# Two more independent products and later turns between output projection and gate/up; first weight sums on VectorE

## The chip, the cores and the metric

The kernel runs on one core of one Trainium2 chip. The metric is the device time of one execution in microseconds (us); of several runs the median counts. The engines are named as in the profile: PE is TensorE (matmuls and transposes), DVE is VectorE, ACT is ScalarE, POOL is GpSimd, SP is the engine whose queue issues the DMAs.

## The reference, cut to what matters

Two layers over 1024 tokens of width 1024, float32. The part around the change:

```python
mixed = jnp.einsum('bse,ed->bsd', jnp.concatenate([tok, mem_out], axis=-1), w_out[i])
x = x + rms_norm(mixed, norm_mix_post[i])
h = rms_norm(x, norm_ffn_pre[i])
gu = jnp.einsum('bsd,df->bsf', h, w_gu[i])          # w_gu: 1024 x 5632
f = jnp.einsum('bsf,fd->bsd', jax.nn.silu(gu[..., :D_FF]) * gu[..., D_FF:], w_down[i])
x = x + rms_norm(f, norm_ffn_post[i])
```

## The kernel before

**Precision.** Every float32 operand is split into a high part (a rounded copy by ScalarE) and a low part (the difference, by VectorE or GpSimd); a product is three matmuls, high x high, low x high, high x low (`mm3`, lines 91 to 93). A 128x128 by 128x512 step is thus three matmuls. `split_raw` (L113) splits a weight unit `wr` of 128x1024 into `wh` (L115) and `wl` (L116); `split_ps` (L95) splits what lies in PSUM.

**Output projection.** The loop of L895 takes the 8 token tiles i one after the other: 48 matmuls into two PSUM banks, then `tail` (L426): squares on ScalarE (L431), `ms` (L161) on VectorE, `r = ms^-0.5` on GpSimd (L165), two scalings (L436), the residual add (L437), the store of x (L424), and `norm_rows` (L173): squares (L176), `ms` (L163), `r`, and the normalised tile `ht` (L178). `turn_tile` (L855) turns a tile: 8 transposes (L186) into the two `pst` banks, and `put_block` copies them to `z` (L838) and splits tokens 0 to 511 into B11 and B21 and the second half of tokens 512 to 1023 into B22. For i >= 4 `combine` (L845) subtracts quarters of `z` in place, four operations of 128x512 on L853, on VectorE for tile 7 and on GpSimd else. In program order the turn of tile i-1 follows the projection of tile i.

**Gate/up.** One level of a Strassen-Winograd scheme: 2x2 blocks of tokens by inner dimension on one side, of weights on the other. A unit f has 7 products of 12 matmuls (`product`, L923): S2·T2, S1·T1, S3·T3, A11·B11, A12·B21, A22·T4 and S4·B22, where A11, A12 are the gate weights, A21, A22 the up weights, S1 to S4 four sums of them (`Sums`, L945, lines 954 to 957) and T1 to T4 what `combine` left in `z`, split in L1063 and L1064. Pieces of S and A22 are split by `piece` (L916). `gate_up` (L977) adds the products up (`add`, L975) and applies Silu. There are 22 units in the order n = 0, 1, 2, ... that is f = 0, 11, 1, 12, ...; weight unit names are w56 and w57 (gate and up of f = 0), w78 and w79 (f = 11), w58 and w59 (f = 1), w80 and w81 (f = 12). The names are those of layer 0. Raw weights come through a ring of two buffers (`load_raw`, L103).

**The junction.** B11 and B21 are complete after tile 3, so products with them can run before tiles 6 and 7 are turned. Lines 1036 to 1053 do this: the gate units w56 and w78 are loaded and split, their A11·B11 and A12·B21 computed into `ahead`, those of w58 into `kept`, the splits of S2, S1, S3, A22, S4 of unit f = 0 made (`A.all()`), and tile 7 turned. The first unit's weight sums run on GpSimd (L1040), into buffers named `attn`. Then T2, T1, T3 and T4 are split, the first two pieces of T2 and of T1 on GpSimd (TPOOL), and the units follow. Unit n = 2 takes its two products from `kept`.

**What sets the order.** Outside the attention a scheduler sorts the instructions of each engine's queue by when it expects them ready; each engine then runs its queue in order and waits on semaphores. DMA issues stand in SP's queue in the same way. Two instructions without a common tile can be ordered by a dependency without a semaphore (`add_manual_dep`).

Of the kernel before, what the change touches and what calls it, by code (L numbers as in the profile page):

```python
# [66 lines left out]
def build(nc, tc, ctx, x_in, mem_in, wts, t5, onehot, sinks, rpb, maskb, gains, out):  # L67
# [105 lines left out]
    def norm_rows(npool, xt, g, nb):  # L173
        ht = npool.tile([P, D], F32, name="ht", tag="ht", bufs=nb)
        ss = npool.tile([P, 1], F32, name="ss", bufs=4)
        nc.scalar.activation(ht, xt, AF.Square, scale=ROOT, accum_out=ss)  # L176
        r = rms(npool, [ss])
        nc.vector.scalar_tensor_tensor(ht, xt, r, g, ALU.mult, ALU.mult)  # L178
        return ht

    def turn(pspool, tag, ht, put):

# [243 lines left out]
    def tail(npool, i, parts, g1, g2, xt, dst, dgrid, nb):  # L426

        tt = npool.tile([P, D], F32, name="tt", tag="ht", bufs=nb)
        ss = npool.tile([P, 2], F32, name="ssp", bufs=4)
        for k, ps in enumerate(parts):  # L430
            nc.scalar.activation(tt[:, k * HALF:(k + 1) * HALF], ps, AF.Square, scale=ROOT,  # L431
                                 accum_out=ss[:, k:k + 1])
        r = rms(npool, [ss[:, 0:1], ss[:, 1:2]])
        for k, ps in enumerate(parts):
            ks = slice(k * HALF, (k + 1) * HALF)
            nc.vector.scalar_tensor_tensor(tt[:, ks], ps, r, g1[:, ks], ALU.mult, ALU.mult)  # L436
        nc.vector.tensor_tensor(xt, xt, tt, ALU.add)  # L437
        store_x(dst, xt, i, dgrid)
        return None if g2 is None else norm_rows(npool, xt, g2, nb)
# [180 lines left out]
    for layer in range(DEPTH):  # L620
# [234 lines left out]
        def turn_tile(i, ht):  # L855
            turn(psT, "pst", ht, put_block(i))
            if i >= 4:
                combine(i - 4)
# [36 lines left out]
        for i in range(NT):  # L895
            accs = [psO.tile([P, HALF], F32, name="acc", tag="acc") for _ in range(2)]
            now_ao, ao = ao, heads_out(i + 1) if i < NT - 1 else None
            xt = load_xt(i)
            for c0 in range(0, 8, 4):
                aH, aL = now_ao[c0 // 4]  # L900
                for c in range(4):
                    h, lo = wu[c0 + c]
                    for dh in range(2):
                        ds = slice(dh * HALF, (dh + 1) * HALF)
                        mm3(accs[dh], aH[:, c], aL[:, c], h[:, ds], lo[:, ds],
                            c0 + c == 0, c0 + c == 7)
            if prev is not None:
                turn_tile(i - 1, prev)
            prev = tail(npool, i, accs, gpost, gpre, xt, x_new, False, 3)
        oph.close()  # L910


        gph = Phase()
        gp = gph.open(sb(f"gu{layer}", side="left"))

        def piece(src):  # L916
            h = gp.tile([P, HALF], F32R, name="gh", tag="gh", bufs=5)
            nc.scalar.activation(h, src, AF.Copy)  # L918
            lo = gp.tile([P, HALF], F32R, name="gl", tag="gl", bufs=5)
            nc.vector.tensor_tensor(lo, src, h.bitcast(F32), ALU.subtract)  # L920
            return h, lo

        def product(A, B):  # L923
            acc = psO.tile([P, HALF], F32, name="acc", tag="acc")
            for kc in range(4):
                ks = slice(kc * P, (kc + 1) * P)
                mm3(acc, A[0][:, ks], A[1][:, ks], B[0][:, kc], B[1][:, kc], kc == 0, kc == 3)
            return acc
# [11 lines left out]
        def gate_unit(f):  # L940
            u = U_GU + 44 * layer + 2 * f
            gr = load_raw(u)
            return gr, split_raw(u, gr, ring, 3)
# [93 lines left out]
        spare = [stage.tile([P, S], F32, name="attn", tag="attn", bufs=2) for _ in range(2)]  # L1037
        spare = [t[:, k * HALF:(k + 1) * HALF] for t in spare for k in range(2)]
        gates = [gate_unit(0)]
        A = Sums(0, gates[0], spare.pop, nc.gpsimd)  # L1040
        gates.append(gate_unit(FH))
        for gate in gates:
            p1 = gp.tile([P, D], F32, name="p1", tag="tw", bufs=2)
# [2 lines left out]
            nc.scalar.activation(p1, product(A11, B11), AF.Copy)  # L1046
            add(c11, product(A12, B21), p1)
            ahead.append((p1, c11))
        gates.append(gate_unit(1))
        A11, A12 = ([t[:, k * HALF:(k + 1) * HALF] for t in gates[2][1]] for k in range(2))  # L1050
        kept = [product(A11, B11), product(A12, B21)]
        A.all()
        turn_tile(NT - 1, prev)
        nph.close()
        stage_ph.close()
        cB = com_ph.open(sb(f"comB{layer}", side="right"))
# [10 lines left out]
        for n in range(NF):  # L1067
            f = n // 2 + n % 2 * FH
            if n:
                gate = gates[n] if n < 3 else gate_unit(f)  # L1070
                if n == 2:
                    gate = load_raw(U_GU + 44 * layer + 2 * f), gate[1]
                A = Sums(f, gate, lambda: tmp("s"), nc.vector)
            if n < 2:
                p1, c11 = ahead[n]
            else:
                p1 = c11 = tmp("e")
                nc.scalar.activation(p1, kept.pop(0) if n == 2 else product(A.A11, B11), AF.Copy)
            act_sums(f, *gate_up(f, A, p1, c11, kept.pop(0) if n == 2 else None))
            if n and summed < FH and summed * (NF - LEAD) <= (n - 1) * FH:  # L1080
                weight_sums(summed)
                summed += 1
# [238 lines left out]
```

## Time and profile before

| | us |
|---|---|
| median of 3 runs | 2269.01 |
| lowest, highest | 2265.79, 2272.14 |
| the profiled execution | 2261.95 |
| its span | 2260.2 |
| PE busy | 2141.8 (95%) |
| DVE busy | 1513.8 (67%) |
| ACT busy | 1064.9 (47%) |
| POOL busy | 726.2 (32%) |

All trace times count from the span's start. A timeline row gives the start of an instruction, its length, its line, output and inputs, and in brackets how long its engine was idle before it and what released it. Rows of one kind that follow each other are one row with xN, whose length spans all of them. Matmuls overlap, so the pace of a row of matmuls is read from their starts. The mean granted TensorE clock is 0.983 of full speed.

### The profile page before, as it was taken

What the parts mean: (1) busy time and instruction counts of PE and PEld (TensorE: products, weight loads), DVE (VectorE), ACT (ScalarE), POOL (GpSimd) and SP (SyncE); (2) the same over time, 40 slices, a digit from 0 to 9 for tenths busy, and PEclk for the clock granted to TensorE, in tenths of its full rate; (3) what the DMA queues carried; (4) which work ended last, traced back from release to release, by engine and by line L of the source; (5) the groups of instructions that cost most, each with busy time, mean ns of one, the idle gap of its engine ahead of it and who ended that gap; (6) DMA issues with size and microseconds to landing.
All of it is one profiled execution on the core that took longest, in us unless ns stands there. A gap on an engine that the chain in (4) does not pass through costs nothing. (4 is left out here: it accounts for less than half of the span.)

```text
span 2260.2 us, 31296 instructions
## 1 busy us (share of the span) xinstructions
PE 2141.8 (95%) x10538; PEld 1779.4 (79%) x10538; DVE 1513.8 (67%) x2629; ACT 1064.9 (47%) x2162; POOL 726.2 (32%) x810
## 2 busy tenths in 40 slices
PE   7899888989999999999899999999899999999986
PEld 7678787768888888887788889777688888888865
DVE  5578785588777765556657665765877777755556
ACT  5488784442233333534457665754523333224333
POOL 3167661424333321102215342524233333211012
PEclk9999999999999999999999999999999999999998
DMA  6433445325555544856333232433255545446664
GB/s 206 118 88 91 135 135 156 98 79 189 175 183 170 180 138 162 276 193 235 114 104 97 78 87 69 132 112 107 75 180 183 184 170 177 145 146 222 193 207 164
DMA packets 152791, 336.49 MB, mean 149 GB/s; under 512 B 24727, under 2 KB 47127, under 8 KB 152632
## 3 DMA queue, kind: packets, MB, share of 16 engines
q1 hardware_dynamic: 152632, 334.50, 46.2%
q8 instruction: 84, 1.38, 0.3%
q14 instruction: 75, 0.61, 0.1%
HBM read 229.06 MB, written 95.03 MB: 143 GB/s over the span
## 5 line engine op out<-in xcount | busy, mean ns | idle before, releaser
L975 DVE TENSOR_TENSOR zt<-acc,zt 128x512 f32<-128x512 f32 x300 | 204.9, 686 | 155.9 <-PE acc L93 153.7
L1120 DVE TENSOR_TENSOR dl<-draw,dh 128x1024 fp32r<-128x1024 f32 x146 | 187.1, 1288 | 163.7 <-ACT dh L1118 163.1
L274 POOL TENSOR_TENSOR sn<-sn,st 128x384 f32<-128x384 f32 (+1 forms) x256 | 188.1, 736 | 254.3 <-DVE st L273 217.7
L1118 ACT ACTIVATE dh<-draw 128x1024 fp32r<-128x1024 f32 x146 | 154.0, 1059 | 218.5 <-PE acc L93 125.8
L92 PE MATMUL acc<-dl,dh 128*128 128x512 f32 x584 | 229.7, 393 | 14.9 <-DVE dl L1120 13.0
L93 PE MATMUL acc<-dh,dl 128*128 128x512 f32 x584 | 228.2, 391 | 0.0
L91 PE MATMUL acc<-dh 128*128 128x512 f32 x584 | 225.3, 391 | 1.3 <-ACT dh L1118 1.2
L918 ACT ACTIVATE gh<-zt 128x512 fp32r<-128x512 f32 x168 | 104.4, 628 | 175.7 <-PE acc L92 156.8
L994 POOL TENSOR_TENSOR tw<-tw 128x512 f32<-128x512 f32 x88 | 131.9, 1499 | 119.1 <-DMA tw<-in_wts 114.2
L1175 POOL TENSOR_TENSOR tt<-tt,g 128x512 f32<-128x512 f32 x32 | 52.2, 1643 | 363.9 <-ACT junk L1174 310.8
L116 DVE TENSOR_TENSOR wl<-wr,wh 128x1024 fp32r<-128x1024 f32 x92 | 118.2, 1285 | 67.3 <-ACT wh L115 65.5
L994 POOL TENSOR_TENSOR zt<-zt 128x512 f32<-128x512 f32 x66 | 90.3, 1368 | 205.1 <-DVE zt L972 201.7
L91 PE MATMUL psg<-hH,wh 128*128 128x512 f32 x384 | 153.1, 399 | 1.8 <-DVE k L229 1.4
L971 ACT ACTIVATE zt<-zt 128x512 f32<-128x512 f32 x84 | 53.1, 632 | 214.7 <-DVE zt L975 214.7
L115 ACT ACTIVATE wh<-wr 128x1024 fp32r<-128x1024 f32 x100 | 105.5, 1055 | 100.5 <-DMA wr<-in_wts 74.9
L92 PE MATMUL psg<-hL,wh 128*128 128x512 f32 x384 | 152.8, 398 | 0.0
L93 PE MATMUL psg<-hH,wl 128*128 128x512 f32 x384 | 152.5, 397 | 0.0
L292 PE MATMUL psv<-PT,v 128*128 128x256 f32 x656 | 143.0, 319 | 5.0 <-DVE attn L667 3.8
L98 DVE TENSOR_TENSOR PT<-pst,PT 128x384 fp32r<-128x384 f32 (+1 forms) x256 | 126.8, 495 | 29.7 <-ACT PT L97 25.1
L92 PEld LDWEIGHTS acc<-dl,dh 128*128 128x128 f32 x584 | 110.0, 188 | 43.3 <-DVE dl L1120 20.7
L272 ACT ACTIVATE sn<-sn,st 128x385 f32<-128x385 f32 (+3 forms) x192 | 113.0, 588 | 60.0 <-DVE st L269 55.7
L920 DVE TENSOR_TENSOR gl<-zt,gh 128x512 fp32r<-128x512 f32 x168 | 129.8, 775 | 7.5 <-ACT gh L918 7.5
(231 smaller groups left out, 5960.1 us busy)
## 6 DMA issues: line engine op xcount, KB each, us to landing
wr<-in_wts SPq DMA_DIRECT2D x146, 512.0 KB
draw<-both_d SPq DMA_DIRECT2D x88, 512.0 KB
both_d<-zt SPq DMA_DIRECT2D x88, 256.0 KB
tw<-in_wts SPq DMA_DIRECT2D x44, 512.0 KB
both_d<-tw SPq DMA_DIRECT2D x44, 512.0 KB
act_d<-zt SPq DMA_DIRECT2D x66, 256.0 KB
draw<-act_d SPq DMA_DIRECT2D x66, 256.0 KB
draw<-in_wts SPq DMA_DIRECT2D x66, 256.0 KB
```

What stands on the lines that cost most here:

```text
L91: nc.tensor.matmul(ps, lh, rh, start=start, stop=False)
L92: nc.tensor.matmul(ps, lh, rl, start=False, stop=False)
L93: nc.tensor.matmul(ps, ll, rh, start=False, stop=stop)
L98: nc.vector.tensor_tensor(ol, ps, oh.bitcast(F32), ALU.subtract)
L116: b = low[0].tensor_tensor(lo, raw, h.bitcast(F32), ALU.subtract)
L274: nc.gpsimd.tensor_tensor(sf, sf, rinv.broadcast_to([P, n]), ALU.mult)
L292: nc.tensor.matmul(pv[:, j % 2], pair.v(self.lo + c)[:, pair.vh + hh], self.PT[:, c], start=c == 0, stop=c == nk - 1)
L920: nc.vector.tensor_tensor(lo, src, h.bitcast(F32), ALU.subtract)
L975: nc.vector.tensor_tensor(o, a, b, ALU.add)
L994: nc.gpsimd.tensor_tensor(o, a, b, ALU.subtract)
L1118: nc.scalar.activation(h, raw, AF.Copy)
L1120: eng.tensor_tensor(lo, raw, h.bitcast(F32), ALU.subtract)
```

## The change

- The turn of tile 6 is taken out of the projection loop and stands behind the products of w56, that of tile 7 behind the products of w78 (`turn_tile(NT - 3 + len(ahead), ...)`).
- A22 of unit f = 0 is split right after its weight sums; the other four splits are made after the turn of tile 6 in program order, and each is tied behind the last norm (`behind`, with `normed[0]`, which is tile 7's `ht`).
- The first weight sums are made by VectorE in place of GpSimd.
- After w58's products two more are done ahead, A11·B11 and A12·B21 of unit n = 3 (f = 12, w80), into the two `pst` banks. Unit n = 3 then takes them from `kept`, and its gate weights are loaded a second time for its sums, as was done for n = 2.

```diff
@@ -175,8 +175,15 @@
         ss = npool.tile([P, 1], F32, name="ss", bufs=4)
         nc.scalar.activation(ht, xt, AF.Square, scale=ROOT, accum_out=ss)
         r = rms(npool, [ss])
-        nc.vector.scalar_tensor_tensor(ht, xt, r, g, ALU.mult, ALU.mult)
+        normed[0] = nc.vector.scalar_tensor_tensor(ht, xt, r, g, ALU.mult, ALU.mult)
         return ht
+
+    normed = [None]
+
+    def behind(ins, first):
+
+        tc.add_manual_dep(ins.ins, first.ins.name, mybir.DependencyInfo(
+            mybir.DependencyClass.NoSync, mybir.DependencyReason.DATA), reason="queued behind")
 
     def turn(pspool, tag, ht, put):
 
@@ -904,24 +911,29 @@
                         ds = slice(dh * HALF, (dh + 1) * HALF)
                         mm3(accs[dh], aH[:, c], aL[:, c], h[:, ds], lo[:, ds],
                             c0 + c == 0, c0 + c == 7)
-            if prev is not None:
+            if prev is not None and i < NT - 1:
                 turn_tile(i - 1, prev)
-            prev = tail(npool, i, accs, gpost, gpre, xt, x_new, False, 3)
+            before, prev = prev, tail(npool, i, accs, gpost, gpre, xt, x_new, False, 3)
         oph.close()
 
 
         gph = Phase()
         gp = gph.open(sb(f"gu{layer}", side="left"))
+
+        late = []
 
         def piece(src):
             h = gp.tile([P, HALF], F32R, name="gh", tag="gh", bufs=5)
             nc.scalar.activation(h, src, AF.Copy)
             lo = gp.tile([P, HALF], F32R, name="gl", tag="gl", bufs=5)
-            nc.vector.tensor_tensor(lo, src, h.bitcast(F32), ALU.subtract)
+            b = nc.vector.tensor_tensor(lo, src, h.bitcast(F32), ALU.subtract)
+            for ins in late:
+                behind(b, ins)
             return h, lo
 
-        def product(A, B):
-            acc = psO.tile([P, HALF], F32, name="acc", tag="acc")
+        def product(A, B, acc=None):
+            if acc is None:
+                acc = psO.tile([P, HALF], F32, name="acc", tag="acc")
             for kc in range(4):
                 ks = slice(kc * P, (kc + 1) * P)
                 mm3(acc, A[0][:, ks], A[1][:, ks], B[0][:, kc], B[1][:, kc], kc == 0, kc == 3)
@@ -1037,7 +1049,8 @@
         spare = [stage.tile([P, S], F32, name="attn", tag="attn", bufs=2) for _ in range(2)]
         spare = [t[:, k * HALF:(k + 1) * HALF] for t in spare for k in range(2)]
         gates = [gate_unit(0)]
-        A = Sums(0, gates[0], spare.pop, nc.gpsimd)
+        A = Sums(0, gates[0], spare.pop, nc.vector)
+        A.A22
         gates.append(gate_unit(FH))
         for gate in gates:
             p1 = gp.tile([P, D], F32, name="p1", tag="tw", bufs=2)
@@ -1046,11 +1059,23 @@
             nc.scalar.activation(p1, product(A11, B11), AF.Copy)
             add(c11, product(A12, B21), p1)
             ahead.append((p1, c11))
-        gates.append(gate_unit(1))
-        A11, A12 = ([t[:, k * HALF:(k + 1) * HALF] for t in gates[2][1]] for k in range(2))
-        kept = [product(A11, B11), product(A12, B21)]
-        A.all()
-        turn_tile(NT - 1, prev)
+            turn_tile(NT - 3 + len(ahead), before if len(ahead) == 1 else prev)
+            if len(ahead) == 1:
+                late.append(normed[0])
+                A.all()
+                late.clear()
+
+        def first_two(f, make):
+            gates.append(gate_unit(f))
+            A11, A12 = ([t[:, k * HALF:(k + 1) * HALF] for t in gates[-1][1]] for k in range(2))
+            kept.append([make(A11, B11), make(A12, B21)])
+
+        def turned_bank():
+            return psT.tile([P, 4, P], F32, name="pst", tag="pst").rearrange("p k t -> p (k t)")
+
+        kept = []
+        first_two(1, product)
+        first_two(FH + 1, lambda A, B: product(A, B, turned_bank()))
         nph.close()
         stage_ph.close()
         cB = com_ph.open(sb(f"comB{layer}", side="right"))
@@ -1067,16 +1092,17 @@
         for n in range(NF):
             f = n // 2 + n % 2 * FH
             if n:
-                gate = gates[n] if n < 3 else gate_unit(f)
-                if n == 2:
+                gate = gates[n] if n < 4 else gate_unit(f)
+                if n in (2, 3):
                     gate = load_raw(U_GU + 44 * layer + 2 * f), gate[1]
                 A = Sums(f, gate, lambda: tmp("s"), nc.vector)
             if n < 2:
                 p1, c11 = ahead[n]
             else:
                 p1 = c11 = tmp("e")
-                nc.scalar.activation(p1, kept.pop(0) if n == 2 else product(A.A11, B11), AF.Copy)
-            act_sums(f, *gate_up(f, A, p1, c11, kept.pop(0) if n == 2 else None))
+                two = kept.pop(0) if kept else [product(A.A11, B11), None]
+                nc.scalar.activation(p1, two[0], AF.Copy)
+            act_sums(f, *gate_up(f, A, p1, c11, None if n < 2 else two[1]))
             if n and summed < FH and summed * (NF - LEAD) <= (n - 1) * FH:
                 weight_sums(summed)
                 summed += 1
```

The new functions `first_two` and `turned_bank` stand whole in the diff. Where instructions of the junction of layer 0 stand on TensorE and VectorE, in the order of each queue:

TensorE before, from the last projection matmul to T2. `ht_5371` is tile 6, `ht_5461` tile 7; wh/wl56, 78 and 58 are the high and low gate weights of units f = 0, 11 and 1.

```order
L93 MATMUL acc_5380<-wh47_4617,aoL_5284 128x512
L186 MATMUL pst_5431<-ident_63,ht_5371 128x128 x4
L186 MATMUL pst_5437<-ident_63,ht_5371 128x128 x4
L91 MATMUL acc_5494<-B11H_4593,wh56_5477 128x512
...
L93 MATMUL acc_5537<-B21H_4595,wl78_5490 128x512
L186 MATMUL pst_5603<-ident_63,ht_5461 128x128 x3
L91 MATMUL acc_5557<-B11H_4593,wh58_5553 128x512
...
L186 MATMUL pst_5609<-ident_63,ht_5461 128x128 x4
L93 MATMUL acc_5557<-B11H_4593,wl58_5554 128x512
...
L93 MATMUL acc_5570<-B21H_4595,wl58_5554 128x512
L91 MATMUL acc_5667<-T2H_5626,gh_5587 128x512
```

TensorE now (lines are shifted: L193 is L186 of before; `ht_5443` is tile 7, `wh80` the gate weights of f = 12).

```order
L93 MATMUL acc_5380<-wh47_4617,aoL_5284 128x512
L91 MATMUL acc_5480<-B11H_4593,wh56_5459 128x512
...
L93 MATMUL acc_5494<-B21H_4595,wl56_5460 128x512
L193 MATMUL pst_5508<-ident_63,ht_5371 128x128 x4
L193 MATMUL pst_5514<-ident_63,ht_5371 128x128 x4
L91 MATMUL acc_5543<-B11H_4593,wh78_5475 128x512
...
L193 MATMUL pst_5571<-ident_63,ht_5443 128x128 x4
L193 MATMUL pst_5577<-ident_63,ht_5443 128x128 x4
L91 MATMUL acc_5595<-B11H_4593,wh58_5591 128x512
...
L93 MATMUL acc_5595<-B11H_4593,wl58_5592 128x512
...
L91 MATMUL pst_5627<-B11H_4593,wh80_5623 128x512
...
L93 MATMUL pst_5640<-B21H_4595,wl80_5624 128x512
L91 MATMUL acc_5699<-T2H_5658,gh_5526 128x512
```

Tile 6's turn stands behind 24 more matmuls than before; tile 7's stands behind w78's products as before, but whole, where four matmuls of w58 cut into it; and 24 matmuls of w80 into `pst` banks stand between w58 and T2.

VectorE before, from tile 7's residual add to the first T2 split (`gl` are low halves of the pieces of unit f = 0, `attn` its weight sums).

```order
L437 TENSOR_TENSOR xt_5381<-xt_5381,tt_5449 128x1024
L920 TENSOR_TENSOR gl_5585<-wr57_5481,gh_5583 128x512
L920 TENSOR_TENSOR gl_5589<-attn_5474,gh_5587 128x512
...
L920 TENSOR_TENSOR gl_5597<-attn_5473,gh_5595 128x512
L178 SCALAR_TENSOR_TENSOR ht_5461<-xt_5381,r_5466,g_6_4613 128x1024
L975 TENSOR_TENSOR p1_5493<-acc_5508,p1_5493 128x512
L920 TENSOR_TENSOR gl_5601<-attn_5473,gh_5599 128x512
...
L116 TENSOR_TENSOR wl58_5554<-wr58_5551,wh58_5553 128x1024
L853 TENSOR_TENSOR zh_4592<-zh_4592 128x512 x2
L98 TENSOR_TENSOR B22L_4598<-pst_5609,B22H_4597 128x4x128
...
L1064 TENSOR_TENSOR T2L_5627<-zh_4592,T2H_5626 128x4x128
```

VectorE now (L444 is L437 of before, L929 L920, L987 L975, L1089 L1064).

```order
L929 TENSOR_TENSOR gl_5471<-wr57_5463,gh_5469 128x512
L444 TENSOR_TENSOR xt_5381<-xt_5381,tt_5431 128x1024
...
L987 TENSOR_TENSOR p1_5479<-acc_5494,p1_5479 128x512
L178 SCALAR_TENSOR_TENSOR ht_5443<-xt_5381,r_5448,g_6_4613 128x1024
L929 TENSOR_TENSOR gl_5528<-attn_5456,gh_5526 128x512
L98 TENSOR_TENSOR B22L_4598<-pst_5514,B22H_4597 128x4x128
...
L929 TENSOR_TENSOR gl_5540<-attn_5455,gh_5538 128x512
L116 TENSOR_TENSOR wl58_5592<-wr58_5589,wh58_5591 128x1024
...
L98 TENSOR_TENSOR B22L_4598<-pst_5577,B22H_4597 128x4x128
...
L1089 TENSOR_TENSOR T2L_5659<-zh_4592,T2H_5658 128x4x128
...
L116 TENSOR_TENSOR wl80_5624<-wr80_5621,wh80_5623 128x1024
```

The split of A22 (`gl` of `wr57`) moved ahead of tile 7's residual add, of the other four, three stood ahead of tile 7's norm and one behind it, now all four stand behind it; `wl58` stays behind them, the last `B22L` of tile 6 stands among them, and `wl80` is new among the T2 splits. On GpSimd the four weight sums are gone, and the `zh` subtractions of tile 6's turn stand behind the last `r` instead of ahead of it. On SP the load of `wr58` moved ahead of tile 7's store, and a load of `wr80` is new behind that store.

## Rows read from the trace of the kernel before

**Rows 1.** The page: busy time, share of the span and instructions.
```profile
PE 2141.8 (95%) x10538; PEld 1779.4 (79%) x10538; DVE 1513.8 (67%) x2629; ACT 1064.9 (47%) x2162; POOL 726.2 (32%) x810
```

**Rows 2.** PE timeline, layer 0: start us, us, engine line op xcount [idle <-releaser].
```profile
444.26 0.39 PE L93 MATMUL acc<-wh,aoL 128*128 128x512 f32 x1
446.54 1.06 PE L186 MATMUL pst<-ident,ht 128*128 128x128 f32 x8 [1.89 <-DVE ht L178]
447.36 0.48 PE L91 MATMUL acc<-B11H,wh 128*128 128x512 f32 x1
...
452.92 0.39 PE L91 MATMUL acc<-B11H,wh 128*128 128x512 f32 x1
...
460.53 0.52 PE L186 MATMUL pst<-ident,ht 128*128 128x128 f32 x3 [2.01 <-DVE ht L178]
463.13 0.80 PE L91 MATMUL acc<-B11H,wh 128*128 128x512 f32 x1 [2.08 <-ACT wh L115]
...
475.08 0.77 PE L92 MATMUL acc<-T2L,gh 128*128 128x512 f32 x1 [3.86 <-DVE T2L L1064]
...
479.91 0.50 PE L91 MATMUL acc<-T1H,gh 128*128 128x512 f32 x1
```

**Rows 3.** Windows: busy us (instructions), granted clock, DMA share, GB/s.
```profile
470.00:480.00 10.00, 6.14 (x18) 4.56 (x17) 10.00 (x12) 6.51 (x13) 4.39 (x3) 0.67 0.01 2
...
490.00:500.00 10.00, 10.00 (x44) 8.05 (x43) 9.88 (x16) 2.93 (x5) 1.29 (x1) 1.00 0.48 160
```

**Rows 4.** PE timeline, the same place in layer 1.
```profile
1577.82 0.39 PE L93 MATMUL acc<-wh,aoL 128*128 128x512 f32 x1
...
1612.25 0.63 PE L91 MATMUL acc<-T1H,gh 128*128 128x512 f32 x1
```

**Rows 5.** POOL timeline, 431 to 457 us.
```profile
431.71 1.31 POOL L954 TENSOR_TENSOR attn<-wr 128x512 f32<-128x512 f32 x1 [1.94 <-DVE aoL L875]
...
436.91 0.56 POOL L165 TENSOR_TENSOR r<-ms,mhalf 128x1 f32<-128x1 f32 x1
...
450.23 6.61 POOL L853 TENSOR_TENSOR zh<-zh 128x512 f32<-128x512 f32 x4
```

**Rows 6.** DVE timeline, 415 to 525 us.
```profile
416.15 0.15 DVE L163 TENSOR_SCALAR ms<-ss 128x1 f32<-128x1 f32 x1 [1.22 <-ACT ht L176]
417.04 1.28 DVE L178 SCALAR_TENSOR_TENSOR ht<-xt,r,g 128x1024 f32<-128x1024 f32 x1 [0.73 <-POOL r L165]
...
437.50 1.41 DVE L436 SCALAR_TENSOR_TENSOR tt<-acc,r,g 128x512 f32<-128x512 f32 x2 [3.18 <-POOL r L165]
...
441.10 2.32 DVE L116 TENSOR_TENSOR wl<-wr,wh 128x1024 fp32r<-128x1024 f32 x1
...
448.33 1.23 DVE L116 TENSOR_TENSOR wl<-wr,wh 128x1024 fp32r<-128x1024 f32 x1 [1.93 <-ACT wh L115]
...
452.22 1.77 DVE L437 TENSOR_TENSOR xt<-xt,tt 128x1024 f32<-128x1024 f32 x1
453.92 1.78 DVE L920 TENSOR_TENSOR gl<-wr,gh 128x512 fp32r<-128x512 f32 x1
...
457.98 0.68 DVE L920 TENSOR_TENSOR gl<-attn,gh 128x512 fp32r<-128x512 f32 x1
...
494.85 1.25 DVE L954 TENSOR_TENSOR zt<-wr 128x512 f32<-128x512 f32 x1
...
506.75 0.69 DVE L954 TENSOR_TENSOR zt<-wr 128x512 f32<-128x512 f32 x1
...
524.77 0.68 DVE L954 TENSOR_TENSOR zt<-wr 128x512 f32<-128x512 f32 x1
```

**Rows 7.** The SP queue's own timeline.
```profile
443.50 0.33 SPq L105 DMA_DIRECT2D wr<-in_wts  x1
```

**Rows 8.** ACT timeline.
```profile
447.24 1.06 ACT L115 ACTIVATE wh<-wr 128x1024 fp32r<-128x1024 f32 x1 [4.87 <-PE pst L186]
```

**Rows 9.** Source line L437: duration ns min/median/max, first and last start us.
```profile
L437 DVE TENSOR_TENSOR xt<-xt,tt x16: 1215/1218/1781, 368.7 to 1585.7; 128x1024 f32<-128x1024 f32 x16
```

## The prediction, written before the changed kernel ran

> **What bounds the kernel now.** I read the page first: TensorE is busy for 95% of the span [rows 1], so a change pays only where TensorE stands still or runs slowly, and the timeline of TensorE shows where that is around the edit. In layer 0 the last output-projection matmul starts at 444.26 and the first T1 matmul at 479.91, 35.65 us later [rows 2]. Between them stand two turns (0.8 us each) and 84 matmuls (24 for each of w56, w78 and w58, 12 of T2). Twenty-four matmuls take 452.92 - 447.36 = 5.56 us [rows 2], 0.232 each, so 84 take 19.5; with the turns and the last projection matmul's own 0.23 the work is 21.3, and 14.3 us are lost. Four idle times are listed: 1.89 and 2.01 for VectorE's `ht`, 2.08 for `wh`, 3.86 for `T2L`, in sum 9.84 [rows 2]. The other 4.5 are slow stretches: in 470 to 480 the granted clock is 0.67 [rows 3], and the 11 T2 matmuls behind the wait take 479.91 - 475.08 = 4.83 instead of 2.55 [rows 2], 0.44 each, which is half pace, the 1.2 GHz level, right after the wait of 3.86. In that window VectorE is busy 10.00 of 10 and TensorE 6.14 [rows 3]: VectorE's queue sets the end of the junction. Layer 1 has the same picture in 1612.25 - 1577.82 = 34.43 us [rows 4], so 1.2 less is lost there.
>
> **The change, part by part.**
>
> *Weight sums on VectorE.* GpSimd does the four sums from 431.71 to 436.91, one after the other, and only then computes `r` for tile 6 [rows 5], for which VectorE waits 3.18 us until 437.50 [rows 6]. On VectorE an operation of this shape takes 0.60 from one start to the next (0.69 long, [rows 6] at 506.75), so the four take some 2.5 and are done by 434.2, before tile 6's `ms`, beside projection matmuls; cost on the path 0. `r` then follows as it does elsewhere (0.15 for `ms`, 0.73 idle for `r`, 416.15 and 417.04 in [rows 6]), and the residual chain starts at 435.15, not 437.50: all that hangs on it is 2.35 earlier. The low half of w56 ends at 441.1 instead of 443.4 [rows 6], w78's load is issued at 441.15 instead of 443.50 [rows 7], and, as before, 3.74 later (447.24 - 443.50) ScalarE begins `wh78` [rows 7, 8], with `wl78` done at 447.2.
>
> *Turn of tile 6 behind w56's products.* These need only B11, B21 and w56, all there at 444.5. TensorE goes straight on; the wait of 1.89 goes. `ht` of tile 6 is normalised in 442.8 to 444.0, long before its turn at 450.1 to 450.9. w78's products follow to 456.4, nothing waiting.
>
> *Tile 7's norm and the splits behind it.* VectorE's residual add of tile 7 begins 2.35 earlier than 452.22 [rows 6], at 449.9, and takes 1.22 instead of 1.77, since GpSimd's `zh` subtractions, which began at 450.23 [rows 5], now come after the later turn 6 (1.22 is L437's median, [rows 9]). The last `r` is there 2.1 after that (1.22 for ScalarE's squares, 0.15, 0.73, by 416.15 and 417.04 in [rows 6]): 453.2. Right behind this `r` GpSimd's queue now has the four `zh` subtractions of turn 6, and the norm's last step reads two tiles from SBUF just then. Where such a pair met before, VectorE's operation was longer by about the rest of a GpSimd one: `wl` 2.32 against 1.23, `gl` 1.78 against 0.68 [rows 6], 1.1 in both. I charge 1.1 to the norm, and 1.1 to each `gl` and to `wl58` while GpSimd still has three `zh` subtractions and two `T2L` to do: `ht` (1.2) ends at 455.5, the first moved split (0.6) at 457.2, `B22L` at 457.8 (it reads PSUM and lets half of a GpSimd operation pass, so the next `gl` pays 0.5), the other three `gl` at 458.9, 460.6 and 462.3, and `wl58` (1.2), which stands behind them, at 464.7. That is 6.0 of meetings (five of 1.1, one of 0.5). Bounds: with none, `wl58` is 6.0 earlier; if each costs a whole spacing of GpSimd's (6.61/4 = 1.65, [rows 5]) it is 3.3 later (six times 0.55). I take 1.1, which is what both nearest rows show.
> By the Trainium skill ("SBUF — State Buffer", section "Who interferes with whom") the port pair of VectorE and GpSimd is an exclusive lock, and who starts first stops the other for its whole instruction; at its word each meeting would cost up to the 1.31 of a GpSimd operation instead of 1.1, some 1.2 us more in each layer, 2261 in all. The trace agrees in kind, with 1.1 us measured.
>
> *Turn of tile 7 and w58.* The turn can start at 456.3 behind w78's products; its second half needs the bank that `B22L` of tile 6 frees at 457.8, so it ends at 458.2. Two w58 matmuls follow, to 458.65; the third reads `wl58` and waits until 464.75: **6.1 us in one piece**, where 2.01, 2.08 and 3.86 stood. Then 22 matmuls take 5.1, plus the slow pace after a long wait: the T2 matmuls lost 4.83 - 2.55 = 2.28 after a wait of 3.86 [rows 2]; the waits of 2.01 and 2.08 together left the two w58 matmuls and the turn behind them slow too. I take 1.4 to 2.3. They end at 471.2 to 472.1.
>
> *Two more products, w80.* Its load waits for the ring buffer that `wl58` frees, at 464.75; 3.74 later [rows 7, 8] `wh80` starts, `wl80` is done at 470.8, just in time. The 24 matmuls take 5.56, to some 477. They are moved, not added: unit n=3 has 60 matmuls instead of 84. Under them VectorE and GpSimd finish T2's splits, so that the wait of 3.86 has cover. The gate weights of w80 are loaded a second time, 512 KB in each layer on the same queue; DMA engines are busy for 0.48 in 490 to 500 [rows 3], so I cost it at 0; uncovered it would be 3.7 each. Without a wait T2's 12 matmuls (2.78) bring T1 to 479.6 to 480.5, say 480.0.
>
> *Sum.* T1 starts when it did, with 5.56 us of unit n=3 already done. Losses tell the same: before 14.3, now 1.0 for the bank, 6.1 for `wl58` and 1.4 to 2.3 of slow pace, 8.5 to 9.4: a gain of 4.9 to 5.8. I take 5.4 in layer 0 and, since 1.2 less was lost there, 4.2 in layer 1: 9.6, **10 us** rounded: the profiled execution goes from 2261.95 (its span 2260.2) to 2252. It lies 7.06 under the median of the runs, 2269.01; taken from that, 2259.0.
>
> **Rivals.**
>
> *A: GpSimd is out of the way.* Its subtractions start late enough, or VectorE's norm begins first, so that three of the six operations pass without a meeting: 3.3 less in each layer, a gain of 16.6 in all, 2252.5; with no meeting at all it would be 12 more than forecast, 2247. For it: the `r` and the norm are released almost together, and 457.98 shows a `gl` at 0.68 [rows 6]. Against: the four subtractions lasted 6.61 beside such work [rows 5], so some overlap is all but sure.
>
> *B: the new wait is dearer.* All 22 matmuls of w58 stay at half pace (0.44 a matmul as in T2 against 0.23, 4.6 in all, a further 2.3 to 3.2 in a layer), or meetings cost 1.65 and `wl58` is 3.3 later. The gain is then 2 to 6, 2264, within what can be told from no change: a measurement of this kernel tells about 0.3%, 6.8 us. For it: w80's load starts only when `wl58` is done, and the chain to `wl80` has no slack by my sum.
>
> *C: VectorE bounds units n=1 to 3, slower.* Each of them now needs only 60 matmuls, 13.9 us, with VectorE's work per unit unchanged. From one unit's first sum to the next VectorE took 506.75 - 494.85 = 11.9, but 524.77 - 506.75 = 18.0 when weight sums ran on GpSimd [rows 6]; it is busy 9.88 of 10 there [rows 3]. VectorE's lead is some 7 us by my estimate (unit 0's 48 matmuls from T1 on take 11.1, the next unit's sums and first split and what stands between them, seven at 0.6, take 4.2); with it, three units at x cost 3(x - 13.9) - 7 in a layer: the gain is used up at x = 17.9; slower by over 6.8 begins at 19.1, and 20 gives 2282. Against: the step before that of 18.0 was 11.9, so that the pace does not last.
>
> *D: no effect.* The waits only change place and sum to the same, 2269.
>
> **How the numbers follow.** Forecast 0.46 (gains of 7 to 13), A 0.17, B 0.27, C 0.06, D 0.04. Faster by over 0.3% is forecast, A and a little of B: 0.65; within it the rest of B, and D: 0.29; slower C: 0.06. The range takes the forecast, most of A and most of B: 2251 to 2266; it leaves out C, D and the tails.
>
> **What would show it.** Right: no idle time before w56's first matmul; `ms` of tile 6 near 434 and no L954 group on GpSimd; tile 7's norm some 2.4 long; one wait of about 6 us in w58 for `wl`, with a lower clock behind it; no wait for `T2L`; T1 at about 480 with w80's products done; units n=1 to 3 without gaps on TensorE. Wrong: a second wait at w80's first matmuls (B), a wait for `wl58` under 3 us (A), or waits for `gl` in units 1 to 3 (C).

## The result, and the profile after

The changed kernel takes 2256.85 us (median of 5 runs, 2251.34 to 2259.36), the kernel before 2267.79 beside it: a ratio of 0.9948, 95% interval 0.9931 to 0.9964, 10.9 us faster. A second set of runs gave 2253.94 against 2265.91, the ratio again 0.9948 (0.9934 to 0.9963). The forecast was 10 us faster, 2259.0 in 2251 to 2266. The profiled execution took 2253.81 (before 2261.95), and TensorE's busy time is what it was [rows 1]:

```profile
PE 2141.3 (95%) x10538; PEld 1780.9 (79%) x10538; DVE 1520.4 (68%) x2637; ACT 1064.0 (47%) x2162; POOL 715.8 (32%) x802
```

TensorE's timeline around the junction of layer 0 in the changed kernel, as in [rows 2]:

```profile
446.92 0.39 PE L93 MATMUL acc<-wh,aoL 128*128 128x512 f32 x1
447.14 0.39 PE L91 MATMUL acc<-B11H,wh 128*128 128x512 f32 x1
...
452.63 1.04 PE L193 MATMUL pst<-ident,ht 128*128 128x128 f32 x8
...
460.37 0.66 PE L193 MATMUL pst<-ident,ht 128*128 128x128 f32 x4 [0.80 <-DVE B22L L98]
...
467.00 0.80 PE L93 MATMUL acc<-B11H,wl 128*128 128x512 f32 x1 [5.50 <-DVE wl L116]
467.59 0.63 PE L91 MATMUL acc<-B11H,wh 128*128 128x512 f32 x1
468.02 0.63 PE L92 MATMUL acc<-B11L,wh 128*128 128x512 f32 x1
...
479.60 0.39 PE L91 MATMUL acc<-T2H,gh 128*128 128x512 f32 x1
...
482.40 0.39 PE L91 MATMUL acc<-T1H,gh 128*128 128x512 f32 x1
```

All of it stands 2.66 later than before (446.92 against 444.26), which has another cause, below. Call **J** the time from the last projection matmul's start to the first T1 matmul's: 482.40 - 446.92 = 35.48, before 35.65, but now with 24 matmuls of w80 in it. The four waits of before are gone; in their place stand one of 0.80 for the bank that `B22L` frees and one of 5.50 for `wl` of w58, with matmuls 0.43 apart behind it (half pace; the granted clock is 0.50 from 467.60 to 471.00, which is the 1.2 GHz level). T2 starts without a wait. In layer 1 the large wait is 4.46 [rows 4]:

```profile
1575.83 0.39 PE L93 MATMUL acc<-wh,aoL 128*128 128x512 f32 x1
...
1594.87 0.79 PE L93 MATMUL acc<-B11H,wl 128*128 128x512 f32 x1 [4.46 <-DVE wl L116]
...
1609.60 0.39 PE L91 MATMUL acc<-T1H,gh 128*128 128x512 f32 x1
```

Windows of the changed kernel: the granted clock falls to 0.73 in 460 to 470, where TensorE is busy 4.13 of 10, and VectorE 9.89; further on TensorE stays full, 10.00 of 10 in every such window from 480 to 550, although VectorE is 10.00 busy in 520 to 530 [rows 3].

```profile
460.00:470.00 10.00, 4.13 (x13) 3.11 (x14) 9.89 (x10) 3.03 (x6) 5.56 (x4) 0.73 0.18 52
...
520.00:530.00 10.00, 10.00 (x44) 8.06 (x44) 10.00 (x11) 2.00 (x4) 6.53 (x5) 1.00 0.49 190
```

VectorE's timeline in the changed kernel (the rows that answer to [rows 6]; `attn` is a weight sum, `gl` a split, L443 the scaling of tile 6 or 7):

```profile
436.33 0.69 DVE L969 TENSOR_TENSOR attn<-wr,attn 128x512 f32<-128x512 f32 x1
...
437.76 1.41 DVE L443 SCALAR_TENSOR_TENSOR tt<-acc,r,g 128x512 f32<-128x512 f32 x2 [0.67 <-POOL r L165]
...
454.90 0.15 DVE L163 TENSOR_SCALAR ms<-ss 128x1 f32<-128x1 f32 x1 [1.22 <-ACT ht L176]
...
455.71 2.31 DVE L178 SCALAR_TENSOR_TENSOR ht<-xt,r,g 128x1024 f32<-128x1024 f32 x1
457.94 1.78 DVE L929 TENSOR_TENSOR gl<-attn,gh 128x512 fp32r<-128x512 f32 x1
...
460.24 4.50 DVE L929 TENSOR_TENSOR gl<-attn,gh 128x512 fp32r<-128x512 f32 x3
464.67 2.28 DVE L116 TENSOR_TENSOR wl<-wr,wh 128x1024 fp32r<-128x1024 f32 x1
...
472.89 1.80 DVE L1089 TENSOR_TENSOR T2L<-zh,T2H 128x512 fp32r<-128x512 f32 x1
```

GpSimd there, in the place of [rows 5]:

```profile
455.13 0.55 POOL L165 TENSOR_TENSOR r<-ms,mhalf 128x1 f32<-128x1 f32 x1 [4.63 <-DVE ms L163]
455.64 6.88 POOL L860 TENSOR_TENSOR zh<-zh 128x512 f32<-128x512 f32 x4
462.75 3.12 POOL L1089 TENSOR_TENSOR T2L<-zh,T2H 128x512 fp32r<-128x512 f32 x2 [0.22 <-ACT T2H L1088]
```

### The profile page after: what moved, and what is told of

Read it like the earlier page. It is cut to its first block, busy times and chain, and to the rows that moved or that the text cites. A ratio compares the mean times of both kernels' runs of the same rounds, so it can differ in the third digit from the quotient of the medians.

```text
span 2251.8 us, 31282 instructions
## 1 busy us (share of the span) xinstructions
PE 2141.3 (95%) x10538; PEld 1780.9 (79%) x10538; DVE 1520.4 (68%) x2637; ACT 1064.0 (47%) x2162; POOL 715.8 (32%) x802
## 5 line engine op out<-in xcount | busy, mean ns | idle before, releaser
L987 DVE TENSOR_TENSOR zt<-acc,zt 128x512 f32<-128x512 f32 x298 | 203.7, 686 | 147.4 <-PE acc L93 145.5
L929 DVE TENSOR_TENSOR gl<-zt,gh 128x512 fp32r<-128x512 f32 x168 | 132.2, 787 | 6.8 <-ACT gh L927 6.5
```

The source lines that it names most:

```text
L929: b = nc.vector.tensor_tensor(lo, src, h.bitcast(F32), ALU.subtract)
L987: nc.vector.tensor_tensor(o, a, b, ALU.add)
```

## The experiments

The table gives J in both layers (from each run's TensorE timeline), and J less 5.56 where w80's 24 matmuls are in it, so that all rows do the same work; the matmuls and turns alone are 21.3. Times with an interval are medians of 4 runs or more, the others one run each. Every J is read from one profiled execution; the two of the changed kernel differ by 0.4 and 1.2.

| kernel | J, layer 0 / 1 | J for equal work | us | ratio to before |
|---|---|---|---|---|
| before | 35.65 / 34.43 | 35.65 / 34.43 | 2264 to 2268 | 1 |
| changed | 35.48 / 33.77 | 29.92 / 28.21 | 2256.85 | 0.9948 (0.9931 to 0.9964) |
| changed, again (e12) | 35.11 / 34.99 | 29.55 / 29.43 | 2253.94 | 0.9948 (0.9934 to 0.9963) |
| sums on GpSimd (e1) | 38.38 / 38.14 | 32.82 / 32.58 | 2264.1 | one run |
| no w80 ahead (e2) | 30.82 / 30.74 | 30.82 / 30.74 | 2256.5 | 0.9967 (0.9955 to 0.9978) |
| tile 6's subtractions left out (e3) | 29.19 / 29.12 | 23.63 / 23.56 | 2242.86 | one run |
| wl58 ahead of the splits (e4) | 33.11 / 33.76 | 27.55 / 28.20 | 2251.41 | 0.9952 (0.9937 to 0.9967) |
| before + sums on VectorE (e5) | 32.13 / 32.07 | 32.13 / 32.07 | 2257.69 | one run |
| early turn 6 (e6) | 33.03 / 34.58 | 27.47 / 29.02 | 2250.91 | one run |
| no tie (e7) | 30.59 / 30.50 | 25.03 / 24.94 | 2244.19 | 0.9904 (0.9883 to 0.9925) |
| no tie, subtractions on VectorE (e8) | 33.50 / 31.00 | 27.94 / 25.44 | 2247.33 | 0.9914 (0.989 to 0.9937) |
| no tie, no w80 (e9) | 28.80 / 28.85 | 28.80 / 28.85 | 2252.44 | 0.9935 (0.9913 to 0.9957) |
| no tie, wl58 ahead of S4 (e10) | 28.41 / 28.30 | 22.85 / 22.74 | 2241.72 | 0.9894 (0.9879 to 0.991) |
| no tie, early turn 6 (e11) | 34.59 / 34.62 | 29.03 / 29.06 | 2252.53 | one run |

**e1: the sums back on GpSimd.**

```diff
-        A = Sums(0, gates[0], spare.pop, nc.vector)
+        A = Sums(0, gates[0], spare.pop, nc.gpsimd)
```

> The changed kernel with one part undone: the first weight sums are again made by GpSimd. J is the time from the start of the last output-projection matmul to the start of the first T1 matmul of layer 0; it is 35.65 in the kernel before and 35.48 in the changed one, which has 24 more matmuls (5.56 us) in it. My theory (VectorE's chain through tile 6, tile 7's norm, the splits and wl58 sets the wait in w58): r of tile 6 comes some 2.4 us later, everything behind it too, the wait for wl58 grows from 5.50 to about 7.9 and J to about 37.8. Rival (the later turns alone remove the waits, the place of the sums does not matter): wait about 5.5, J about 35.5.

J is 38.38, near the 37.8 of the theory, but the wait for `wl58` did not take the difference. The wait at the junction's start stays away (TensorE goes from the last projection matmul at 447.50 to w56 at 447.72), so the later turn of tile 6 removes it by itself. TensorE waits for tile 7's `ht` and longer for the bank first:

```profile
461.18 0.63 PE L193 MATMUL pst<-ident,ht 128*128 128x128 f32 x4 [1.48 <-DVE ht L178]
463.37 0.66 PE L193 MATMUL pst<-ident,ht 128*128 128x128 f32 x4 [1.56 <-DVE B22L L98]
...
470.02 0.80 PE L93 MATMUL acc<-B11H,wl 128*128 128x512 f32 x1 [5.53 <-DVE wl L116]
```

1.48, 1.56 and 5.53 here, nothing, 0.80 and 5.50 in the changed kernel: the whole chain is later, and TensorE pays at the first place that reads it. The sums are worth 2.9 and 4.4 us by J against the changed kernel's first run, 3.3 and 3.2 against its second (e12).

**e2: w80's products not ahead.**

```diff
         first_two(1, product)
-        first_two(FH + 1, lambda A, B: product(A, B, turned_bank()))
...
-                gate = gates[n] if n < 4 else gate_unit(f)
+                gate = gates[n] if n < 3 else gate_unit(f)
-                if n in (2, 3):
+                if n == 2:
```

> The changed kernel with one part undone: the two products of unit n=3 (w80) stay in their unit and are not done ahead. The prediction's step (w80's products cover the wait of 3.86 for T2L and the slow pace behind it): that wait comes back after w58's products, J is 29.9 plus 4 to 6, that is 34 to 36, and with 5.56 still to do in unit n=3 a layer is 4 to 6 slower, the median about 2265 to 2269. Rival, from the trace of the changed kernel (the last T2L ends at 474.69 and w58's last matmul at about 474.05, and without wl80 the split is 1.2 earlier): there is nothing to cover any more, T2 follows w58 without a wait, J is 29.9 to 30.4 and the median is that of the changed kernel, about 2257.

The rival's way: after the wait of 5.51 for `wl58` there is none for `T2L`.

```profile
464.89 0.80 PE L93 MATMUL acc<-B11H,wl 128*128 128x512 f32 x1 [5.51 <-DVE wl L116]
...
473.05 0.39 PE L92 MATMUL acc<-T2L,gh 128*128 128x512 f32 x1
```

For equal work J is 0.9 and 2.5 longer than in the changed kernel (1.3 and 1.3 against its second run, e12). Much of that is not T2's: 12 and 11 matmuls ran 0.43 apart here, 9 and 5 there, 0.2 us each, and in layer 1 the wait for `wl58` is 5.52 against 4.46. The interval of the ratio, 0.9955 to 0.9978, overlaps the changed kernel's. With w58 late, T2's splits are done before TensorE gets to T2 (the last ends at 469.65 + 0.68 = 470.33, T2 starts at 472.82), and w80's products have nothing to cover.

**e3: tile 6's four GpSimd subtractions left out** (their results are missing from a quarter of the tokens' T blocks).

```diff
-            if i >= 4:
+            if i >= 4 and i != 6:
                 combine(i - 4)
```

> The changed kernel without GpSimd's four zh subtractions of token tile 6 in both layers; they are left out, so the T blocks of a quarter of the tokens hold other numbers. My theory (the meetings of VectorE's operations with these four cost five times 1.1 and more): tile 7's ht takes 1.28 instead of 2.31, the gl splits 0.6 each instead of 1.5, wl58 is done about 5 us earlier, the wait for it is 0 to 0.7, no half pace behind it, and J falls from 35.48 to about 29. Rival (VectorE's own work sets the wait, meetings move it little): the wait stays above 4, J above 34.

The theory's numbers, on VectorE's timeline of this run:

```profile
455.59 1.29 DVE L178 SCALAR_TENSOR_TENSOR ht<-xt,r,g 128x1024 f32<-128x1024 f32 x1
456.79 0.68 DVE L929 TENSOR_TENSOR gl<-attn,gh 128x512 fp32r<-128x512 f32 x1
...
458.00 1.88 DVE L929 TENSOR_TENSOR gl<-attn,gh 128x512 fp32r<-128x512 f32 x3
459.80 1.22 DVE L116 TENSOR_TENSOR wl<-wr,wh 128x1024 fp32r<-128x1024 f32 x1
```

```profile
461.07 0.50 PE L93 MATMUL acc<-B11H,wl 128*128 128x512 f32 x1 [0.70 <-DVE wl L116]
...
468.03 0.50 PE L93 MATMUL pst<-B11H,wl 128*128 128x512 f32 x1 [1.22 <-DVE wl L116]
```

`ht` takes 1.29 against 2.31, the split behind it 0.68 against 1.78, the three splits 1.88 against 4.50, `wl58` 1.22 against 2.28: 1.0 + 1.1 + 2.6 + 1.1 = 5.8. In the changed kernel `wl58` met not the subtractions, which end at 455.64 + 6.88 = 462.52, but the two `T2L` splits behind them, from 462.75 to 465.87; here GpSimd starts these at 461.71, when `wl58` is done. So the 5.8 is what GpSimd's work in this stretch costs as a whole, not the four subtractions alone. TensorE's wait falls from 5.50 to 0.70, another of 1.22 comes at `wl80`, and no matmul runs at half pace. J falls by 6.3 and 4.7.

**e4: wl58 ahead of the four splits.**

```diff
-                late.append(normed[0])
+                gates.append(gate_unit(1))
+                late.extend((normed[0], low_last[0]))
...
-            gates.append(gate_unit(f))
+            if f != 1:
+                gates.append(gate_unit(f))
```

(`low_last[0]` is the last low split made, here wl58's.)

> The changed kernel with wl58 queued ahead of the four moved splits, which are tied behind it. If only the place of wl58 in VectorE's queue makes the wait (theory 1), wl58 is done at about 460.8 on the changed kernel's scale, the wait of 5.50 and the half pace behind it go, J falls by 5 to 7 to about 29, and the median by 10 to 14, to about 2245. If VectorE's queue as a whole is the bound (theory 2), the wait goes to w80's products, whose low half wl80 stands behind the splits and the zh subtractions: w58 waits 0 to 0.5, w80's third matmul about 4.5, J is 34 to 35, and the median within 3 us of the changed kernel's.

Theory 2: w58 runs through, and the wait stands at w80, whose `wl` is behind the splits and three `zh` subtractions.

```profile
472.97 0.80 PE L93 MATMUL pst<-B11H,wl 128*128 128x512 f32 x1 [4.59 <-DVE wl L117]
```

J is 2.4 and 0.0 shorter than in the changed kernel's first run, a little under the 34 to 35 expected; the ratio is 0.9952, against 0.9948. Moving one item up a full queue moved the wait one item down.

**e5: the sums alone**, in the kernel before.

```diff
-        A = Sums(0, gates[0], spare.pop, nc.gpsimd)
+        A = Sums(0, gates[0], spare.pop, nc.vector)
```

> The kernel before with one part of the change alone: the first weight sums on VectorE. J (last output-projection matmul to first T1 matmul) was 35.65 in layer 0 and 34.43 in layer 1. My theory: r of tile 6 and all behind it come some 2.4 us earlier, the wait of 1.89 at the start of the junction goes, the others keep their size, J is about 33.3 and 32.1. Rival (the sums only matter together with the later turns): the time moves into the next wait, J stays within 0.7 of the kernel before.

J is 32.13 and 32.07, shorter by 3.5 and 2.4: the theory's way, with 1.2 more than expected in layer 0, where 9 matmuls instead of 13 ran at half pace. The wait at the junction's start is gone with the early turn still in place; the other three are 1.68, 2.08, 3.98 in layer 0 (1.27, 2.08, 2.60 in layer 1):

```profile
458.86 0.52 PE L186 MATMUL pst<-ident,ht 128*128 128x128 f32 x3 [1.68 <-DVE ht L178]
461.46 0.79 PE L91 MATMUL acc<-B11H,wh 128*128 128x512 f32 x1 [2.08 <-ACT wh L115]
...
473.39 0.47 PE L92 MATMUL acc<-T2L,gh 128*128 128x512 f32 x1 [3.98 <-DVE T2L L1064]
```

These 5.9 us are half of what the whole change gives in the two junctions (35.65 - 29.92 = 5.7 and 34.43 - 28.21 = 6.2).

**e6: tile 6 turned where it was.**

```diff
-            if prev is not None and i < NT - 1:
+            if prev is not None:
                 turn_tile(i - 1, prev)
...
-            turn_tile(NT - 3 + len(ahead), before if len(ahead) == 1 else prev)
+            if len(ahead) == 2:
+                turn_tile(NT - 1, prev)
```

> The changed kernel with one part undone: the turn of tile 6 stands where it stood, right behind the last projection tile; all else stays. If the later turn is what removes the wait at the start (the prediction's step), that wait of about 1.9 comes back and J rises from 35.48 to about 37. Rival, from the changed trace: with the sums on VectorE tile 6's ht ends 0.5 before the projection does, so the turn waits for nothing; GpSimd's four zh subtractions then run before the last r instead of beside tile 7's norm and the splits, and that is worth more than what they delay r by: wl58 is done some 4 us earlier on the common scale, the wait for it is 1 to 3, J 30.5 to 32.

No wait at the start, so with the sums on VectorE the later turn is not needed to remove it. GpSimd's subtractions run before the last `r`, and VectorE's norm and the four splits and `wl58` behind it pass without meetings:

```profile
457.13 1.28 DVE L178 SCALAR_TENSOR_TENSOR ht<-xt,r,g 128x1024 f32<-128x1024 f32 x1 [1.62 <-POOL r L165]
...
458.93 2.49 DVE L929 TENSOR_TENSOR gl<-attn,gh 128x512 fp32r<-128x512 f32 x4
461.34 1.22 DVE L116 TENSOR_TENSOR wl<-wr,wh 128x1024 fp32r<-128x1024 f32 x1
```

`wl58` ends 462.56 - 446.45 = 16.1 after the last projection matmul, against 20.0 in the changed kernel. J is 2.4 shorter in layer 0 (33.03, a little above the rival's 30.5 to 32) and 0.8 longer in layer 1 than the first run of the changed kernel, or 2.1 and 0.4 shorter than its second: waits for `wh` (1.54) and for `wl80` (1.6 to 1.9) came in.

**e7: no tie behind the norm.**

```diff
             if len(ahead) == 1:
-                late.append(normed[0])
                 A.all()
```

> The changed kernel with one part undone: the four splits are not tied behind tile 7's norm, so that three of them stand ahead of its ms, while VectorE waits for ScalarE's squares, and ahead of GpSimd's subtractions. My theory (meetings and the queue behind the norm make the wait for wl58): ht is 0.6 later, but three splits take 0.6 each and are off the queue; wl58 is done near 462.5 on the changed kernel's scale instead of 466.95, the wait for it falls from 5.50 to 1 to 2, J to 30 to 31.5, the median by 8 to 11 against the changed kernel, to about 2247. Rival (the tie is needed, since splits ahead of the norm hold up tile 7's turn): a wait for ht of about 2 at turn 7, J above 34, the median no better than the changed kernel's.

The theory's numbers. Three splits now fill the time in which VectorE waited 1.22 for ScalarE's squares, and GpSimd is idle beside them:

```profile
455.11 1.89 DVE L929 TENSOR_TENSOR gl<-attn,gh 128x512 fp32r<-128x512 f32 x3
...
457.73 2.30 DVE L178 SCALAR_TENSOR_TENSOR ht<-xt,r,g 128x1024 f32<-128x1024 f32 x1
...
460.55 1.17 DVE L929 TENSOR_TENSOR gl<-attn,gh 128x512 fp32r<-128x512 f32 x1
461.65 2.29 DVE L116 TENSOR_TENSOR wl<-wr,wh 128x1024 fp32r<-128x1024 f32 x1
```

```profile
463.99 0.50 PE L93 MATMUL acc<-B11H,wl 128*128 128x512 f32 x1 [2.02 <-DVE wl L116]
```

The four splits take 1.89 + 1.17 here, 1.78 + 4.50 where all stand behind the norm; the norm starts some 0.5 later on J's scale, the wait is 2.02. J falls by 4.9 and 3.3 (4.5 and 4.5 against the changed kernel's second run), the median by some 10 us, the ratio to 0.9904; its interval lies wholly below the changed kernel's.

**e8: the same, with tile 6's subtractions on VectorE.**

```diff
-            eng = nc.vector if i == 3 else nc.gpsimd
+            eng = nc.vector if i >= 2 else nc.gpsimd
```

> As the last one, and tile 6's four zh subtractions on VectorE instead of GpSimd: 2.4 us of work more in VectorE's queue, no meetings with them. If a meeting costs what the trace says (ht 1.0, a split 1.1, wl58 1.1), this takes 3 to 4 out and puts 2.4 in, so that J is 29 to 30.5, 0.5 to 1.5 better than without it, the median 2245 to 2247. Rival (VectorE's work alone counts): J is 2.4 worse than without it, about 33.

Neither: J is 2.9 and 0.5 longer than in e7. The wait for `wl58` falls to 0.53 and 0.69, but one of 2.99 and 3.06 comes at `wl80`, behind eight subtractions:

```profile
468.05 0.79 PE L93 MATMUL pst<-B11H,wl 128*128 128x512 f32 x1 [2.99 <-DVE wl L116]
...
1594.64 0.50 PE L93 MATMUL pst<-B11H,wl 128*128 128x512 f32 x1 [3.06 <-DVE wl L116]
```

In layer 0 12 matmuls follow at half pace, in layer 1 none, which is the difference of 2.5 between the two. The medians of e7 and e8 can't be told apart.

**e9: neither the tie nor w80's products ahead** (e7 with e2's edit).

> The kernel without the tie of the splits (J 30.59 and 30.50, median 2244.2), and also without w80's products ahead; with e2 this makes a two by two of tie and w80. My theory (w80's products are worth something only where w58 is no longer late): w58's last matmul is now followed by T2, whose last split ended at 475.03 in that run, 4.5 after w58's products did, and is 1.2 earlier without wl80: a wait of 3 to 3.5 for T2L and half pace behind it come back, J is 28.5 to 30.5 instead of the 25.0 that 30.59 - 5.56 would be, and the median rises by 7 to 11, to about 2251 to 2255. Rival (w80's products are worth as little as with the tie, 1 to 2 a layer): J 25 to 27, median 2245 to 2248.

The wait of 2.92 for `T2L` is back, where e2, with the tie, had none:

```profile
460.73 0.50 PE L93 MATMUL acc<-B11H,wl 128*128 128x512 f32 x1 [1.82 <-DVE wl L116]
...
469.95 0.47 PE L92 MATMUL acc<-T2L,gh 128*128 128x512 f32 x1 [2.92 <-DVE T2L L1087]
```

For equal work J is 3.8 and 3.9 longer than in e7. So w80's products cover what the prediction said they cover, once w58 is not late; behind the tie they are worth 0.9 to 2.5, most of it the half pace and the wait for `wl58` of e2.

**e10: no tie, and wl58 ahead of S4's split.**

```diff
...
-                late.append(normed[0])
+                A.S2, A.S1, A.S3
+                gates.append(gate_unit(1))
+                late.append(low_last[0])
                 A.all()
...
```

> The kernel without the tie, and wl58 ahead of the one split that still stood between the norm and it (S4, needed last of all). My theory: wl58 ends 1.1 earlier, its wait falls from 2.0 to about 0.9, w80's load is issued 1.1 earlier too, J is 29 to 29.8, the median 2 to 3 lower, 2241 to 2243 (little for a median). Rival (the port meeting moves on to wl58): the wait stays at 2.

```profile
459.70 0.50 PE L93 MATMUL acc<-B11H,wl 128*128 128x512 f32 x1 [0.41 <-DVE wl L117]
...
466.22 0.50 PE L93 MATMUL pst<-B11H,wl 128*128 128x512 f32 x1 [0.74 <-DVE wl L117]
```

Two waits of 0.41 and 0.74, and no half pace at all: J is 28.41 and 28.30, below what was expected since the half pace of e7 (8 and 7 matmuls) went too. For equal work that is 22.8, 1.5 above the bare 21.3. The median of 2241.72 is 24 us below the kernel before, 0.9894 (0.9879 to 0.991): the best version found, by J (2.2 shorter than e7 in both layers); the intervals of the two ratios overlap.

**e11: no tie, and tile 6 turned early** (e7 with e6's edit).

> The kernel without the tie, and the turn of tile 6 back behind the last projection tile (so the change is only the sums, w80 and tile 7's whole turn). GpSimd's subtractions then run before the last r. If the later turn of tile 6 pays by itself once the tie is gone: J is 2 or more above 30.6, with a wait for ht at tile 7's turn of 1.3 to 1.7, as where the sums alone were changed, and one for wh58 behind it. Rival (the place of turn 6 does not matter, as the run with the tie and the early turn showed 33.0 against 35.5): J within 1.5 of 30.6.

The rival fell. Without the tie the early turn costs 4.0 and 4.1: GpSimd's four subtractions stand before the last `r`, beside the splits ahead of the norm (2.38 for two), and tile 7's `ht` is 1.73 late again.

```profile
455.85 2.38 DVE L929 TENSOR_TENSOR gl<-attn,gh 128x512 fp32r<-128x512 f32 x2
...
459.33 1.28 DVE L178 SCALAR_TENSOR_TENSOR ht<-xt,r,g 128x1024 f32<-128x1024 f32 x1 [0.44 <-POOL r L165]
```

So the later turn of tile 6 pays where the splits are not tied, while with the tie it cost 2.1 to 2.4 in layer 0 and made no clear difference in layer 1 (e6): the two edits of the change work against each other. J is from one execution each here.

**e12: the changed kernel again.**

> The changed kernel once more, for how far J and the time ahead of the junction repeat. Its program ahead of the junction is the same, in the same order, as before; the last output-projection matmul of layer 0 started at 446.92 against 444.26. If that is variation from run to run, it starts anywhere in 444 to 449 here; if the change causes it, at 446.9 within 0.3. J is expected at 35.5 and 33.8 to 35.5, the wait for wl58 at 4.5 to 5.5.

```profile
448.43 0.39 PE L93 MATMUL acc<-wh,aoL 128*128 128x512 f32 x1
...
468.51 0.80 PE L93 MATMUL acc<-B11H,wl 128*128 128x512 f32 x1 [5.52 <-DVE wl L116]
```

The last projection matmul starts at 448.43, in the twelve runs between 444.80 and 449.32: variation of a part that no edit touches, and what the first profile was late by. The waits repeat (5.52 and 4.46), J does within 1.2, by the half pace behind the wait (9 and 5 matmuls in the first run, 7 and 11 here).

## Why the prediction was right, and where not

Right in sign and size (forecast 10, measured 10.9 and 12.0) and in the chain that sets the one large wait, the norm, the splits and `wl58` beside GpSimd. Two steps gave a reason that the runs do not bear out: the later turn of tile 6 and w80's cover. The gains by layer are off by up to 2.0 us, and J of the changed kernel itself differs by 1.2 between two executions, so an agreement closer than that is luck.

- *Sums on VectorE*: done at 437.02 - 2.66 = 434.4 (forecast 434.2), tile 6's scaling at 437.76 - 2.66 = 435.1 (435.15). By e5 (5.9 of 11.9 in the two junctions) and e1 (7.3, or 6.5 against the second run) this is half of the gain or more.
- *Turn of tile 6*: "the wait of 1.89 goes" held, but the prediction gives the later turn as the reason, and that was not needed. Either edit removes the wait alone: e1 loses it by the later turn, e5 and e6 lose it with the early one, by the sums. What the later turn adds behind the sums is to move GpSimd's subtractions behind the last `r`, where by the prediction's own charge they meet the norm, the splits and `wl58`; what they would cost before it was not asked, and by e6 that is less in layer 0 while, without the tie, by e11 it is more.
- *Meetings*: `ht` 2.31 (forecast 2.4 in all), `wl58` done at 466.95 - 2.66 = 464.3 (464.7), the sum of meetings 5.8 by e3 (6.0). The norm, the first split and `wl58` each paid 1.0 to 1.1, the other three splits 2.6 together. GpSimd's first subtraction starts at 455.64 and the norm at 455.71, and the norm is 1.0 longer; GpSimd was held up too: its four lasted 6.88, where an estimate from the 1.31 of a weight sum of the same shape [rows 5] is 5.2. By the Trainium skill ("SBUF — State Buffer", section "Who interferes with whom") the one that starts first holds the shared ports for its whole instruction; the trace agrees in kind, and for the size the measured 1.0 to 1.1 decides. In layer 1 one meeting fewer took place (the three splits took 3.43, not 4.50) and the wait was 4.46, not 5.50.
- *Wait in w58*: 5.50 and 0.80 for the bank (6.1 and 1.0); the half pace lost 9 x 0.2 = 1.8 (1.4 to 2.3).
- *w80*: T1 at 482.40 - 2.66 = 479.7 (480.0). The step "the wait of 3.86 has cover" failed as an explanation: T2's last split ends at 472.89 + 1.80 = 474.69 and T2 starts at 479.60. The late w58 had already taken the time; e2 shows no wait without w80, e9 the wait once w58 is early. The sum was right all the same, since it set all the waits that go against the one that comes.
- *Sum*: 5.7 us in layer 0 (forecast 5.4) and 6.2 in layer 1 (4.2), together 11.9; layer 1 was low by the missing meeting (1.0) and a short half pace. The second run gave 6.1 and 5.0. The first profiled pair differs by 8.1 in own time only, as 2.66 came ahead of the junction and 1.4 in the down projection of layer 0, where no instruction was moved.
- *Rivals*: A (fewer meetings) held for one operation of layer 1. B's late `wl80` did not come, and C's waits in units 1 to 3 did not either: TensorE is full in every window from 480 to 550. What the prediction did not see is that the tie itself costs: it put the splits where GpSimd works and took them from where VectorE stood idle for 1.22, which is 3.3 to 4.9 a layer by e7.

## What to carry to other kernels

When one engine's queue sets the end of a stretch, an item pulled ahead or tied back moves the wait along the queue; list what stands behind it and who reads that, before counting the old wait as gained. Short work belongs where its engine waits anyway and where the engine that holds it up is idle: three splits took 1.89 there, three behind the norm 4.50. Parts of a change should be timed singly and in pairs: here half the gain came from one word, one part was worth little until another was undone, and the best version left the tie behind the norm out.

## What was not expected of the hardware

The half pace after a wait of one size is not of one length: after 4.46 TensorE ran 5 matmuls at half pace in one run and 11 in the other, after 3.0 in e8 12 in layer 0 and none in layer 1, each 0.2 us longer. The granted clock shows it: 0.50, the 1.2 GHz level, from 1593.60 to 1598.20 in e12 and from 468.70 to 473.60 in e8, but 1.00, the 2.4 GHz level, from 1594.70 to 1600.00 in e8, right after its wait of 3.06. After waits of 0.3 to 1.3 alone (e3, e10) there was none. So two values of J that differ by 1 us may differ in nothing but this, and a wait that goes altogether can return some 2 us more than its length.
